# Seven block products for eight in 13 of 44 pairs of k-tiles of a down projection

## The chip, the core and the metric

The kernel runs on one core of one Trainium2 chip. The metric is the device time of one execution in microseconds. A core has TensorE (matrix products, results into PSUM), VectorE, ScalarE and GpSimd (POOL in the profile) for the other arithmetic, and SyncE, whose queue issues the loads. PSUM has eight banks of 128 x 512 float32 values each.

## The reference

One layer of an encoder block for 256 tokens of width 2048: a mixer, then a gated feed-forward part, then a gated per-layer embedding. The part that changes is the feed-forward part's second product:

```python
def conv_glu(hn, w_up, conv_w, conv_b, w_down):
    up = hn @ w_up
    gate, val = jnp.split(up, 2, axis=-1)
    gate = dwconv_centred(gate, conv_w, conv_b)
    return (jax.nn.gelu(gate, approximate=True) * val) @ w_down
```

`w_down` is 5632 x 2048. The product is 256 tokens by 5632 by 2048, in float32. Its result is normalised by row and added to the residual `h`; then `h`, normalised, is multiplied by `w_ple_gate` (2048 x 2048).

## The kernel before

Float32 products are made from three products of a rounded type (float32r). Each operand is split into a high part (a cast) and a low part (the operand less its high part), and the result is high x high + high x low + low x high. So every block product is three matmuls. The helper `split` (lines 138 to 149) does this for weights: a ScalarE cast into a tile `whi` (names ending in `h`) and a VectorE subtraction into a tile `wlo` (names ending in `l`). There are five buffers of each, and a buffer comes free when TensorE has read it.

The weights come as raw tiles `raw` (lines 151 to 154) of 128 x 2048 values, two k-tiles of 1024 columns, one load of 1 MB each through SyncE's queue, into three buffers. A k-tile is 128 rows of the weight matrix.

The down projection is `sublayer("dn", w_down, ...)` (line 749). It runs over two halves of 1024 output columns. For each half it has four PSUM banks `acc[t][n]`: t is the block of 128 tokens, n the block of 512 columns. They are named `dna` in the profile. `token_major` (lines 201 to 221) runs over 22 pairs of k-tiles. For each it loads the raw tile, splits the two k-tiles and makes 24 matmuls: two k-tiles x two token blocks x three products x two column blocks. They go k-tile by k-tile, except in the last pair, where they go bank by bank, so that the banks end one after the other. `get_hid` (line 730) splits the hidden activations of a pair into a tile `hs` (two buffers): one ScalarE cast and one VectorE subtraction of 512 columns.

At the end of a half each bank is squared and summed by ScalarE (`dnj`, line 669) and multiplied by the gain into the pages `dnm` by VectorE (line 670). After the second half the row factors are worked out on POOL, `h` is updated (line 677), turned by TensorE into PSUM (`dnxt`), and split into `dnxh` and `dnxl` (lines 183 and 184). That panel is the input of the gate product. Between the down projection and the gate stands a small product `ple` of 24 matmuls (line 752).

PSUM is given out from two pools: six banks tagged `main` and two tagged `misc`. The pages of 128 x 2048 values have 13 buffers and the tiles `mid` of 128 x 1024 have three.

The order of the instructions on each engine isn't written out. A scheduler takes the program as the code traces it and sets each engine's order by its own estimates of time, so an instruction may stand earlier or later than in the code. On the chip each engine then takes its instructions strictly in that order.

Of the kernel before, what the change touches and what calls it, by code (L numbers as in the profile page):

```python
# [11 lines left out]
F32 = mybir.dt.float32  # L12
F32R = mybir.dt.float32r
# [3 lines left out]
P = 128  # L17
L = 256
# [5 lines left out]
NF = DFF // P  # L24
# [13 lines left out]
V_FCW, V_PN, V_FCB, V_N = 120, 252, 268, 312  # L38
# [13 lines left out]
def build(nc, a, out):  # L52
    x = a["x"][0]
    w_in, w_out, w_up = a["w_in"][0], a["w_out"][0], a["w_ffn_up"][0]
    w_down, w_gate, w_ple = a["w_ffn_down"][0], a["w_ple_gate"][0], a["w_ple"][0]
    out = out[0]

    with tile.TileContext(nc) as tc, \
# [8 lines left out]
        def ins(r):  # L67
            return getattr(r, "ins", r)

        def page(name, dtype=F32):  # L70
            return gp.tile([P, 2048], dtype, tag="pg", bufs=13, name=name)

        def mid(name, dtype=F32):
            return gp.tile([P, 1024], dtype, tag="mid", bufs=3, name=name)

        def tiny(name, n=2):
            return sp.tile([P, n], F32, tag="tiny", bufs=40, name=name)

        def main(name):
            return [pm.tile([P, 512], F32, tag="main", name=f"{name}_{i}") for i in range(2)]  # L80

        def misc(name):
            return pc.tile([P, 512], F32, tag="misc", name=name)

        def mm(o, lhsT, rhs, start, stop):
            nc.tensor.matmul(o, lhsT, rhs, start=start, stop=stop, skip_group_check=True)  # L86
# [17 lines left out]
        acc, acc2 = [main(f"dtu{t}") for t in range(2)], main("dtu2")  # L104
# [10 lines left out]
        def load(dst, src, ahead=False):  # L115

            with tc.issue_after(last["dma"]) if last and not ahead else nullcontext():
                return ins(nc.sync.dma_start(dst, src))
# [19 lines left out]
        def split(name, src, nel, cuts=()):  # L138

            if name in spare:  # L140
                hi, lo = spare.pop(name)
            else:
                hi = wp.tile([P, 1056], F32R, tag="whi", bufs=5, name=f"{name}h")
                lo = wp.tile([P, 1056], F32R, tag="wlo", bufs=5, name=f"{name}l")
            for c0, c1 in zip((0, *cuts), (*cuts, nel)):
                s = slice(c0, c1)
                last["act"] = ins(nc.scalar.copy(hi[:, s], src[:, s]))
                last["dve"] = ins(nc.vector.tensor_sub(lo[:, s], src[:, s], hi[:, s].bitcast(F32)))  # L148
            return hi, lo

        def raw(name, src, a_, b_):
            r = wp.tile([P, 2048], F32, tag="raw", bufs=3, name=name)
            last["dma"] = load(r[:, :a_ * b_].rearrange("p (a b) -> p a b", a=a_), src, True)
            return r
# [34 lines left out]
        def aside():  # L189

            for job in (work.pop(0) if work else ()):
                job()

        def columns(acc):

            c = 0
            for o in acc:
                yield o, c
                c += o.shape[-1]

        def token_major(name, w, c0, ks, get, acc, tail=1):

            group, nu = [], len(ks) // 2
            for u in range(nu):
                k0 = ks[2 * u]
                r = raw(f"{name}r{k0}", w[k0 * P:(k0 + 2) * P, c0:c0 + 1024]
                        .rearrange("(k p) c -> p k c", p=P), 2, 1024)
                for j in range(2):
                    group.append((k0 + j, *split(f"{name}{k0}_{j}", r[:, j * 1024:(j + 1) * 1024], 1024)))
                if nu - tail <= u < nu - 1:  # L210
                    continue

                order = [(t, o, g, q) for t in range(2) for o in columns(acc[t]) for g in group for q in range(3)] \
                    if u == nu - 1 else \
                    [(t, o, g, q) for g in group for t in range(2) for q in range(3) for o in columns(acc[t])]
                for t, (o, c), (k, wh, wl), q in order:
                    xh, xl = (v[:, t * P:(t + 1) * P] for v in get(k))
                    xx, ww = ((xh, wh), (xh, wl), (xl, wh))[q]
                    mm(o, xx, ww[:, c:c + o.shape[-1]], k == ks[0] and q == 0, k == ks[-1] and q == 2)
                group = []  # L220
                aside()

# [39 lines left out]
        def rms(name, parts, scale, n=1):  # L262

            base = EPS
            for i, q in enumerate(parts):
                m = tiny(f"{name}m{i}", n)
                nc.gpsimd.tensor_scalar(m, q, scale, base, op0=ALU.mult, op1=ALU.add)
                base = m
            r = tiny(f"{name}r", n)
            nc.gpsimd.tensor_tensor(r, m, mhalf[:, :n], op=ALU.pow)  # L270
            return r
# [71 lines left out]
        for u in range(0, NK, 2):  # L343
            r = [wp.tile([P, 2048], F32, tag="raw", bufs=3, name=f"dtur{u}") if u else r0, page(f"dtur{u + 1}")]
            for j in range(2):
                k = u + j
# [17 lines left out]
            for j in range(2):  # L364
                k = u + j
                with tc.issue_after(front[0]), tc.issue_after(front[1]):
                    wh, wl = split(f"dtu{k}", r[j][:, :1056], 1056, ((352, 704), (704,))[k] if k < 2 else ())
                if k == 8:
                    half = last["act"], last["dve"]
# [241 lines left out]
        ])  # L611
        zacc = [main(f"z{t}") for t in range(2)]
        token_major("z", w_in, 0, list(range(NK)), hn, zacc)
        assert not work

# [4 lines left out]
        for t in range(2):  # L620
# [13 lines left out]
            r = rms(f"yn{t}", [ss], rz[t][:, 1:2], n=2)  # L634
# [16 lines left out]
        def gload(name, src):  # L651
            g = cp.tile([P, D], F32, tag="gain", name=name)
            load(g, src.partition_broadcast(P))
            return g

        def sublayer(name, w, ks, get, gain, h, vnext, panel=Panel):

            mg = [page(f"{name}m{t}") for t in range(2)]
            sq = [[], []]
            for half in range(2):  # L660
                acc = [main(f"{name}a{half}{t}") for t in range(2)]
                token_major(f"{name}{half}", w, half * 1024, ks, get, acc)
                for t in range(2):
                    for n in range(2):
                        q = tiny(f"{name}q{t}{half}{n}", 1)
                        junk = sp.tile([P, 512], F32, tag="junk", bufs=1, name=f"{name}j{t}{half}{n}")
                        c = slice(half * 1024 + n * 512, half * 1024 + (n + 1) * 512)
                        b = acc[t][n]
                        nc.scalar.activation(junk, b, AF.Square, accum_out=q)
                        nc.vector.tensor_mul(mg[t][:, c], b, gain[:, c])  # L670
                        sq[t].append(q)
            r = [rms(f"{name}{t}", sq[t], 1.0 / D) for t in range(2)]
            pan = panel(f"{name}x")
            for c in range(4):
                s = slice(c * 512, (c + 1) * 512)
                for t in range(2):
                    nc.vector.scalar_tensor_tensor(h[t][:, s], mg[t][:, s], r[t], h[t][:, s],  # L677
                                                   op0=ALU.mult, op1=ALU.add)
                panel_part(f"{name}x", pan, h, vnext, 4 * c, 4 * c + 4)
            return pan  # L680
# [15 lines left out]
        h = [page(f"h{t}") for t in range(2)]  # L696
# [9 lines left out]
        hid = [page(f"hid{i}") for i in range(6)]  # L706
        for s in range(DFF // 512):
            sc = mid(f"gr{s}")
            for i in range(2):
                ga = main(f"ga{s}{i}")  # L710
                feature_pairs(f"ug{s}{i}", w_up, s * 512 + i * 256, hf, ga)
                o = sc[:, i * 512:(i + 1) * 512]
                total(o, ga)
                v = o.rearrange("p (f t) -> p f t", f=2)
# [5 lines left out]
            for i in range(2):  # L720
                va = main(f"va{s}{i}")
                feature_pairs(f"uv{s}{i}", w_up, DFF + s * 512 + i * 256, hf, va)
                c0 = (s % 2) * 1024 + i * 512
                hd = hid[s // 2][:, c0:c0 + 512]
# [5 lines left out]
        def get_hid(k):  # L730
            if k % 2 == 0:
                t = lp.tile([P, 1024], F32R, tag="hs", bufs=2, name=f"hs{k}")
                src = hid[k // 8][:, (k % 8) * L:(k % 8 + 2) * L]
                nc.scalar.copy(t[:, :512], src)  # L734
                nc.vector.tensor_sub(t[:, 512:], src, t[:, :512].bitcast(F32))
                cur["t"] = t
            o = (k % 2) * L
            return cur["t"][:, o:o + L], cur["t"][:, 512 + o:512 + o + L]
# [3 lines left out]
        def hid_get(k):  # L742
# [3 lines left out]
                hcache[k0], hcache[k0 + 1] = get_hid(k0), get_hid(k0 + 1)  # L746
            return hcache[k]

        hp = sublayer("dn", w_down, list(range(NF)), hid_get, gload("gffn", a["ffn_norm_post"][0]), h, V_PN)


        pl.append(ple(1))
# [32 lines left out]
        for half in range(2):  # L785
            acc = [main(f"gt{half}{t}") for t in range(2)]
# [9 lines left out]
            for t in range(2):  # L796
                for n, (o, c0) in enumerate(columns(acc[t])):
                    c1 = c0 + o.shape[-1]
                    c = slice(half * 1024 + c0, half * 1024 + c1)

                    th = mid(f"gth{half}{t}{n}")
                    v = th[:, :c1 - c0]
# [6 lines left out]
                    q = tiny(f"gq{t}{half}{n}", 1)  # L809
# [53 lines left out]
```

## Time and profile before

| | |
|---|---|
| median of three runs | 1154.63 us (1154.47 to 1155.65) |
| the profiled execution's own time | 1154.53 us |
| its span, first to last instruction | 1152.5 us |
| mean granted TensorE clock | 0.995 |
| TensorE matmuls busy | 1134.8 us |
| VectorE busy | 753.5 us |
| ScalarE busy | 574.7 us |
| down projection, from its first matmul to the next stage's | 800.7 to 1044.75 us |
| loads of a raw tile of `w_down`, issue to landing | 5.5 and 5.6 us |

The profile gives for each engine how long it was busy, and for each instruction when it started, how long it lasted and what ended the idle time before it. PE is TensorE's matmuls, PEld its weight loads, DVE is VectorE, ACT is ScalarE. Instructions of one engine overlap at their ends, so the distance from one start to the next is a little less than the duration shown. A matmul of 128 x 512 is shown with 0.39 us, but in a full stretch one starts every 0.231 us.

### The profile page before, as it was taken

How to read it: one execution, taken by the hardware profiler on the slowest of the kernel's cores; microseconds unless marked ns; L12 is line 12 of the kernel's file. 1: busy time of each engine (PE TensorE's matmuls, PEld its weight loads, DVE VectorE, ACT ScalarE, POOL GpSimd, SP SyncE). 2: the span in 40 equal slices, each digit the busy share in tenths (PEclk: the TensorE clock that was granted, in tenths of full speed). 3: DMA queues.
4: the chain of work that ended last, by engine and by line, in shares of the span. 5: the costliest groups of instructions: out<-in, count | busy, mean ns of one | idle time of the engine just before them, and what ended most of it. 6: DMA issues, size and time to landing. Idle time of an engine off the chain costs nothing.

```text
span 1152.5 us, 15287 instructions
## 1 busy us (share of the span) xinstructions
PE 1134.8 (98%) x6096; PEld 978.4 (85%) x6096; DVE 753.5 (65%) x934; ACT 574.7 (50%) x775; POOL 121.4 (11%) x123
## 2 busy tenths in 40 slices
PE   9998999999999999999999999999999999999996
PEld 9997988888888888888888888888888888887886
DVE  6578896654776666666666766766555565557573
ACT  6533543553675454554544544545444454447462
POOL 0274505200110000000000000000000000001001
PEclk9998999999999999999999999999999999999999
DMA  9952357556456555556555555566666656664652
GB/s 355 337 182 75 109 163 275 184 161 204 144 186 215 186 183 184 191 192 195 189 183 183 188 194 196 183 208 202 187 193 196 191 183 187 191 193 160 221 181 73
DMA packets 129590, 219.02 MB, mean 190 GB/s; under 512 B 3696, under 2 KB 96752, under 8 KB 128624
## 3 DMA queue, kind: packets, MB, share of 16 engines
q1 hardware_dynamic: 129232, 217.70, 57.9%
q8 instruction: 47, 0.77, 0.3%
q10 hardware_dynamic: 288, 0.36, 0.1%
q14 instruction: 23, 0.19, 0.0%
HBM read 215.95 MB, written 2.10 MB: 189 GB/s over the span
## 4 chain that ended last, share of the span: by engine, by line
PE 92%; DVE 5%; ACT 1%; issue 1%; POOL 1%; DMA 0%; DVEq 0%; POOLq 0%; ACTq 0%
PE va L86 21%; PE dna L86 21%; PE ga L86 21%; PE woa L86 8%; PE gt L86 7%; PE dtu L86 4%; PE z L86 4%; PE xbc L86 3%; DVE cv L328 2%; DVE w L541 1%; DVE xb_0l L148 1%; PE ple L86 0%; PE yd L86 0%; DVE h L677 0%; DMA dtur<-w_in 0%
## 5 line engine op out<-in xcount | busy, mean ns | idle before, releaser
L86 PE MATMUL ga<-wox,ug_0h 128*128 128x512 f32 x352 | 125.5, 395 | 0.0
L86 PE MATMUL ga<-wox,ug_1h 128*128 128x512 f32 x352 | 125.1, 394 | 0.0
L86 PE MATMUL va<-wox,uv_0h 128*128 128x512 f32 x352 | 124.8, 393 | 0.0
L86 PE MATMUL va<-wox,uv_1h 128*128 128x512 f32 x352 | 124.8, 393 | 0.0
L86 PE MATMUL dna<-dn_1h,hs 128*128 128x512 f32 x352 | 104.4, 393 | 0.0
L86 PE MATMUL dna<-dn_0h,hs 128*128 128x512 f32 x352 | 104.4, 393 | 0.0
L86 PE MATMUL ga<-wox,ug_0l 128*128 128x256 f32 x352 | 99.1, 282 | 0.0
L86 PE MATMUL ga<-wox,ug_1l 128*128 128x256 f32 x352 | 99.1, 282 | 0.0
L86 PE MATMUL va<-wox,uv_0l 128*128 128x256 f32 x352 | 99.1, 281 | 0.0
L86 PE MATMUL va<-wox,uv_1l 128*128 128x256 f32 x352 | 99.1, 281 | 0.0
L86 PEld LDWEIGHTS dna<-dn_1h,hs 128*128 128x128 f32 x352 | 66.1, 188 | 15.3
L86 PEld LDWEIGHTS dna<-dn_0h,hs 128*128 128x128 f32 x352 | 66.0, 188 | 15.3
L86 PEld LDWEIGHTS va<-wox,uv_0h 128*128 128x128 f32 x352 | 66.1, 188 | 15.0
L86 PEld LDWEIGHTS va<-wox,uv_1h 128*128 128x128 f32 x352 | 66.1, 188 | 15.0
L86 PEld LDWEIGHTS ga<-wox,ug_1h 128*128 128x128 f32 x352 | 66.1, 188 | 14.9
L86 PEld LDWEIGHTS ga<-wox,ug_0h 128*128 128x128 f32 x352 | 66.1, 188 | 14.8
L718 POOL TENSOR_TENSOR fc<-fc,rfb 128x1024 f32<-128x1024 f32 x11 | 26.4, 2404 | 440.1 <-ACT fc L717 440.1
L86 PEld LDWEIGHTS ga<-wox,ug_0l 128*128 128x128 f32 x352 | 66.2, 188 | 0.1
L86 PEld LDWEIGHTS ga<-wox,ug_1l 128*128 128x128 f32 x352 | 66.2, 188 | 0.0
L86 PEld LDWEIGHTS va<-wox,uv_1l 128*128 128x128 f32 x352 | 66.2, 188 | 0.0
L86 PEld LDWEIGHTS va<-wox,uv_0l 128*128 128x128 f32 x352 | 66.2, 188 | 0.0
L734 ACT CAST hs<-hid 128x512 fp32r<-128x512 f32 x44 | 27.3, 620 | 71.1 <-PE dna L86 70.7
(639 smaller groups left out, 2650.5 us busy)
## 6 DMA issues: line engine op xcount, KB each, us to landing
dn0r<-w_ffn_down SPq DMA_DIRECT2D x22, 1024.0 KB, 5.5
dn1r<-w_ffn_down SPq DMA_DIRECT2D x22, 1024.0 KB, 5.6
zr<-w_in SPq DMA_DIRECT2D x8, 1024.0 KB, 5.3
wo0r<-w_out SPq DMA_DIRECT2D x8, 1024.0 KB, 5.7
wo1r<-w_out SPq DMA_DIRECT2D x8, 1024.0 KB, 5.5
gt0r<-w_ple_gate SPq DMA_DIRECT2D x8, 1024.0 KB, 5.8
gt1r<-w_ple_gate SPq DMA_DIRECT2D x8, 1024.0 KB, 5.5
dtur<-w_in SPq DMA_DIRECT2D x14, 528.0 KB, 8.8
```

Of the source, the lines that this page charges most:

```text
L86: nc.tensor.matmul(o, lhsT, rhs, start=start, stop=stop, skip_group_check=True)
L148: last["dve"] = ins(nc.vector.tensor_sub(lo[:, s], src[:, s], hi[:, s].bitcast(F32)))
L328: nc.vector.scalar_tensor_tensor(o[:, lo:hi], i[:, lo + d:hi + d], vec(wcol + j * wstep + f), o[:, lo:hi], op0=ALU.mult, op1=ALU.add)
L541: nc.vector.scalar_tensor_tensor(w[:, h * P:(h + 1) * P], cbm[:, 0, g, t, :], dt[:, t, 8 * g + h:8 * g + h + 1], w[:, h * P:(h + 1) * P], ...
L718: nc.gpsimd.tensor_tensor(cv.rearrange("p (f t) -> p f t", f=4), cv.rearrange("p (f t) -> p f t", f=4), rfb.unsqueeze(1).to_broadcast([P, ...
L734: nc.scalar.copy(t[:, :512], src)
```

## The change

Two k-tiles, two blocks of 128 tokens and two blocks of 512 columns make a product of 2 x 2 blocks by 2 x 2 blocks. Done plainly it has eight block products. In 13 of the 44 pairs (pairs 2, 5, 8, 11, 14 and 17 of each half, and 19 of the second) the kernel after uses Strassen's scheme in Winograd's form, with seven block products. It needs sums and differences of the weight blocks and of the activation blocks.

- `seven_products` forms the weight sums in place in the raw tile by three VectorE subtractions, one 1024 and two 512 columns wide. It splits four pieces in place of two: `a` (512 columns), `b`, `c` and `d` (1024 each); `a` and `b` are taken before the subtractions change their blocks. Then it makes 7 x 3 matmuls. Three products go into the result banks `acc`; four go into four more banks `alt` (named `dns`), where they add up over all fast pairs of the half.
- `hid_sums` forms four sums of activation blocks by four VectorE operations on 128 x 128 values, and splits them (512 columns). For pairs 2, 5, 8 and 11 the split sums are kept in two pages `hsum` for the second half; the others are made in each half (`hd`, `he`).
- `combine` runs once in each half, in the pair after the last fast one. It adds the four shared banks into the result banks in place: one ScalarE copy and eight VectorE additions, four of them with a PSUM bank as input and output. That pair's matmuls go bank by bank, as the last pair's do.
- The banks: half 0 takes two of the six `main` banks and both `misc` banks for `alt`, beside the four of `acc`; half 1 likewise.

The rest of the code is as before. The scheduler sets the order anew. In its new order on VectorE the low split `gt_1l` of the gate's second k-tile stands behind six of the `dnxl` instructions; before it stood ahead of the last `dnm`. In SyncE's queue the load of `gple` stands ahead of the fourth load `gt0r` and not behind it.

```diff
+        def seven_products(name, r, a_, acc, alt, start, stop):
+            v = r.rearrange("p (b c) -> p b c", b=4)
+            b11 = split(f"{name}a", r[:, :512], 512)
+            b2 = split(f"{name}b", r[:, 1024:], 1024)
+            nc.vector.tensor_sub(v[:, 0:2], v[:, 1::2], v[:, 0:2])
+            nc.vector.tensor_sub(v[:, 3], v[:, 3], v[:, 0])
+            nc.vector.tensor_sub(v[:, 2], v[:, 2], v[:, 3])
+            t13 = split(f"{name}c", r[:, :1024], 1024)
+            t42 = split(f"{name}d", r[:, 1024:], 1024)
+            for x, (wh, wl), c, o, own in (
+                    ("a11", b11, 0, alt[0], True), ("a12", b2, 0, acc[0][0], False), ("s4", b2, 512, acc[0][1], False),
+                    ("s1", t13, 0, alt[1], True), ("s3", t13, 512, alt[2], True), ("a22", t42, 0, acc[1][0], False),
+                    ("s2", t42, 512, alt[3], True)):
+                xh, xl = a_[x]
+                for q, (xx, ww) in enumerate(((xh, wh), (xh, wl), (xl, wh))):
+                    mm(o, xx, ww[:, c:c + 512], own and start and q == 0, own and stop and q == 2)
+
+        def combine(name, acc, alt):
+            m = [mid(f"{name}v{i}") for i in range(2)]
+            p1, s16, s165, s167 = (m[i // 2][:, i % 2 * 512:(i % 2 + 1) * 512] for i in range(4))
...
+            nc.scalar.copy(p1, alt[0])
+            add(s16, alt[3], p1)
+            add(acc[0][0], acc[0][0], p1)
+            add(s165, alt[1], s16)
+            add(acc[0][1], acc[0][1], s165)
+            add(s167, alt[2], s16)
+            add(acc[1][0], acc[1][0], s167)
+            add(s165, alt[2], s165)
+            add(acc[1][1], acc[1][1], s165)
...
+                if u in fast:
+                    seven_products(f"{name}{k0}", r, sums(k0), acc, alt, u == fast[0], u == fast[-1])
+                    continue
...
-                    if u == nu - 1 else \
+                    if u == nu - 1 or u - 1 in fast[-1:] else \
...
+                if u - 1 in fast[-1:]:
+                    combine(name, acc, alt)
...
+                alt = main(f"{name}s{half}") if fast[half] and half == 0 else []
                 acc = [main(f"{name}a{half}{t}") for t in range(2)]
+                if fast[half]:
+                    alt += (main(f"{name}s{half}") if half else []) + [misc(f"{name}s{half}_{i}") for i in (2, 3)]
...
+        def hid_sums(k):
+            (h1, l1), (h2, l2) = get_hid(k), get_hid(k + 1)
+            if k not in kept:
...
+                nc.vector.tensor_add(s1, a21, a22)
+                nc.vector.tensor_sub(s3, a11, a21)
+                nc.vector.tensor_sub(s2, s1, a11)
+                nc.vector.tensor_sub(s4, a12, s2)
+                o = keep[-1][:, n % 2 * 1024:(n % 2 + 1) * 1024] if n < 4 else mid(f"he{k}", F32R)
+                nc.scalar.copy(o[:, :512], s[:, :512])
+                nc.vector.tensor_sub(o[:, 512:], s[:, :512], o[:, :512].bitcast(F32))
...
+        hp = sublayer("dn", w_down, list(range(NF)), hid_get, gload("gffn", a["ffn_norm_post"][0]), h, V_PN,
+                      fast=((2, 5, 8, 11, 14, 17), (2, 5, 8, 11, 14, 17, 19)), sums=hid_sums)
```

## The prediction

> **What bounds the kernel now.** I read four views, from the whole to the place of the change. First the engine table of the page, then the chain that ended last: TensorE is busy for 98% of the span and makes 92% of the chain.
>
> ```profile
> PE 1134.8 (98%) x6096; PEld 978.4 (85%) x6096; DVE 753.5 (65%) x934; ACT 574.7 (50%) x775; POOL 121.4 (11%) x123
> PE 92%; DVE 5%; ACT 1%; issue 1%; POOL 1%; DMA 0%; DVEq 0%; POOLq 0%; ACTq 0%
> ```
>
> Then what TensorE waited for in the whole kernel: seven waits, none of them in the down projection. The third lies just behind it, in the first gate matmuls.
>
> ```profile
> PE seg L86 <- DVE catl L184: 5.0, 1, 5.0
> PE gt L86 <- DVE gt_0l L148: 0.7, 1, 0.7
> ```
>
> The two halves of the down projection, in windows (TensorE, weight loads, VectorE, ScalarE, POOL, granted clock, DMA share, GB/s): TensorE never stops, at full clock, and VectorE works 70 of 122 us.
>
> ```profile
> 800.70:922.70 122.00, 122.00 (x530) 99.13 (x529) 70.32 (x70) 58.84 (x73) 0.90 (x2) 1.00 0.61 190
> 922.70:1044.70 122.00, 122.00 (x529) 99.11 (x529) 70.77 (x70) 59.59 (x74) 1.53 (x5) 1.00 0.61 190
> ```
>
> So here each matmul taken out is worth its spacing, as long as VectorE and ScalarE stay ahead. The timeline gives the spacing: the last pair starts at 1039.21 and the next stage's first matmul at 1044.75, 24 matmuls, 0.231 us each. In that pair six in a row go to one bank and are no slower, so three in a row in the new pairs cost nothing extra.
>
> ```profile
> 1039.21 0.39 PE L86 MATMUL dna<-dn_0h,hs 128*128 128x512 f32 x1
> 1044.75 0.40 PE L86 MATMUL ple<-ple_0h,pth 128*128 128x512 f32 x1
> ```
>
> The helpers' rows in the same stage: a 1024-wide VectorE subtraction lasts 1.23 us, and the next starts 1.14 after it (1067.31, 1068.44); a 512-wide one 0.69, next after 0.60. ScalarE's casts: 1.05 (next after 0.96) and 0.62 (0.53).
>
> **The change part by part.**
>
> *Matmuls.* A fast pair has 7 products of 3 matmuls, 21 for 24. 13 pairs make 39 fewer (the built program has 39 fewer): 39 x 0.231 = **-9.0 us**, all on the path.
>
> *A fast pair's helpers.* VectorE: three in-place subtractions (1.14 + 0.60 + 0.60), four low splits (0.60 + 3 x 1.14), the hidden split 0.60: 7.0 us, where an ordinary pair has 2 x 1.14 + 0.60 = 2.9. ScalarE: 0.53 x 2 + 0.96 x 3 = 3.9 for 2.5. TensorE gives it 4.85 us and an ordinary pair 5.54. So VectorE falls behind in a fast pair and recovers in the two ordinary ones: 7.0 + 2 x 2.9 = 12.8, some 13.0 with the waits on its own results, of 15.9 us. What counts is the lead. Splits have five buffers, so each may start when the one five before it has been read (ScalarE starts 0.2 after that). With zero at TensorE's start of a fast pair: next pair's splits done by 2.4 and 3.6, its hidden split by 4.2 (wanted at 5.8); the second's by 5.3, 6.4, 7.0; of the next fast pair a at 7.6, first subtraction 8.8, b 10.1, the other two 11.3, c 13.4, d 15.6. TensorE wants a at 15.9, c at 18.0, d at 19.4. Nearest margin 1.6 us, for d 3.8: cost 0. If that cover were gone, each late microsecond would come back 13 times.
>
> *DMA.* A raw tile is held until d is split, 0.3 us before its pair is consumed; the load three pairs on is issued then and lands at about 5.3 (median 5.5 to 5.6), used from 5.1, while a is wanted at 15.9: cost 0, and 0 at double. SP's order changes in one place, `gple` before the fourth `gt0r` load; that load now waits for the late `gt_1l` below, lands at about 17 and is split after 22: 0.
>
> *Hidden sums.* Nine times four 128x128 operations and one 512-wide, plus a cast. No such sum is in the trace: between 0.23 (the 128x128 copy) and 0.41 (256-wide add); I take 0.25, near the row of its width: 1.6 us each. In the built order they start during the last up-projection step, where VectorE stands idle up to 1.6 us at a time, and end by the first fast pair. The casts into `hsum` wait for pages of `wox` (about 793 and 796) and hold up ScalarE's `dn_1h` from 798.05 to 798.6, wanted at 809. Behind the sums the hidden split of the pair after the first fast one is ready at 816.2, wanted at 817.4: cost 0; at 0.41 the margin is about used up, still 0. The three sums of half 1 lie around the change of halves, ahead of its first fast pair: 0.
>
> *Combine.* Eight VectorE adds per half. Four write SBUF like `dnm` (0.69, next after 0.60); four write PSUM in place, which no row shows: from 0.60 (`dnm` only reads it) to 1.23 (a second pass, the 1024-wide row). I take 0.60. The first needs the fast pair's last product; the others wait for the bank-by-bank pair that follows, and VectorE's splits are queued behind. In the built order TensorE takes the other banks first: bank 1,1 is wanted 7.6 us after that pair begins and its add ends at 6.8; the next hidden split is wanted at 6.9 and ready at 6.25, in half 1 at 7.1 and 6.6. Cost 0, at 1.23 about 1.2 to 1.6 a half, **0 to +2.8**.
>
> *The seam behind it.* The built order moves `gt_1l` (1.14 on VectorE) from ahead of the last `dnm` to behind the sixth `dnxl`. Zero at the first full stretch of `ple` (1044.75 before). VectorE: last `dnm` to 1.9; four `h` of 0.66 to 4.6; two `dnxl` (0.39, waiting for `dnxh`) to 5.75; two `h` to 7.1; two `dnxl` behind ScalarE's `gt_1h` to 8.0; two `h` to 9.3; two `dnxl` to 10.1; `gt_1l` ends 11.3. TensorE: 23 `ple` and 8 transposes to 6.2, eight gate matmuls to 8.0, eight transposes of 0.088 to 8.74, then it needs `gt_1l`: until 11.38, **2.64 us**. The old wait there goes, as VectorE is past `gt_0l` before TensorE is; it cost 1056.59 - 1055.67 (four transposes from 1055.32) = 0.92. Net **+1.7**. Bounds: -0.9 without any wait, +2.5 if the `dnxl` come 0.8 later.
>
> ```profile
> 1055.32 0.60 PE L280 MATMUL dnxt<-ident,h 128*128 128x128 f32 x4
> 1056.59 0.72 PE L86 MATMUL gt<-gt_0l,dnxh 128*128 128x512 f32 x2 [0.67 <-DVE gt_0l L148]
> ```
>
> *Half change.* `dnm` of half 0 ends 2 us ahead of the matmul that needs its bank, though 2.5 us of sums go in ahead of it: 0. Behind the seam the order is the same to the end.
>
> Sum: -9.0 + 1.7 = -7.3. The profiled execution took 1154.53 (span 1152.5 and 2.0 around it), 0.1 under the median of 1154.63: **1147.3 us**.
>
> **The rivals.** Below 0.2% (2.3 us) a measurement of this kernel can't tell a change from none.
>
> *No wait at the seam:* VectorE's chain proves shorter, or TensorE slower to get there. -9.9: 1144.7. Against it: `gt_1l` stands behind six `dnxl` whose inputs come from TensorE itself. 7%.
>
> *The clock falls after the new gap.* The trace has two gaps to compare: after 0.67 us the clock stays 1.00, after 4.95 it is 0.60 and then 0.55 for eight us.
>
> ```profile
> 100.00:104.00 4.00, 1.20 (x3) 1.04 (x4) 3.40 (x7) 2.34 (x4) 0.00 (x0) 0.60 0.80 262
> 104.00:108.00 4.00, 4.00 (x12) 3.15 (x12) 2.34 (x4) 1.28 (x3) 0.70 (x1) 0.55 0.50 135
> ```
>
> A fall like that costs at most 4 x 0.40 + 4 x 0.45 = 3.4: 1150.7. 2.6 is nearer to 0.67. 7%. The Trainium skill, "TensorE: Matmul & The Clock Gate" (HAM oscillation), has the gate close only after gaps over about 3.4 us; by that rule there is no fall here, and the two gaps agree with it.
>
> *TensorE waits for the combine:* the in-place adds cost 1.23. +2.8: 1150.1. For it: all eight banks are held and no row shows the operation. Against: the PSUM read is free (0.69 in `dnm`, 0.69 in `hs`). 11%. The Trainium skill, "Perfetto Trace Analysis" (Optimizing Tensor Performance), wants matmul groups to rotate through banks so that one is emptied under the next; here the groups go on in the banks being added to, and by that rule this rival is the likely one. No row of this trace decides it; the built order gives TensorE other banks first.
>
> *VectorE becomes the bound, and the kernel slower.* Place: the fast pairs. 13.0 us of VectorE per 15.9: from 1.22 times dearer on TensorE waits, and from 1.27 times (0.56 a period, 13 periods) the 7.3 are gone. The trace has such a factor: `z_1l` takes 1641 ns, the same subtraction as `dn_1l` at 1226, 1.34 times. At 1.34, 13.0 grows to 17.4, 1.5 late in 13 periods: 1147.3 + 19 = 1166, less if the leads cushion it. Against: the long ones stand where POOL works, and POOL has 0.9 and 1.5 us in the down projection's halves; the change gives it nothing. 7%.
>
> That the change doesn't do what it says is excluded by the 39.
>
> **How the numbers follow.** Likeliest, seam wait and all else hidden: 63%, 1147.3. The cases above take 7, 7, 11 and 7%; 5% is several at once. The range reaches from no seam wait (1144.5) to past the clock's fall (1151.0) and leaves VectorE's case and the mixtures out. Faster 0.88 (all but those), same 0.05 (mixtures), slower 0.07.
>
> **What the profile after would show.** Right: TensorE solid from `dna`'s start to its end, the stage about 235 us long with 1017 matmuls; one wait of `gt` for `gt_1l` of 2.3 to 2.6 us in place of that for `gt_0l`; VectorE near 85% busy. Wrong: waits of `dns` or `dna` for low splits at every fast pair (VectorE), one per half for an add (combine), a clock under 1.00 after 1040, or several waits at the seam.

## The result and the profile after

The kernel after takes 1146.65 us (median, 1146.28 to 1147.28) where the kernel before takes 1154.58 (1154.47 to 1155.65). The ratio is 0.9931, 95% interval 0.9918 to 0.9943: 0.7% faster. The profiled execution of the kernel after took 1147.28 us, with a span of 1145.5; that is 7.25 us less than the profiled execution of before (1154.53), and the prediction was 7.3 less. Between the medians the difference is 7.9; the profiled execution is the slowest of the four.

The first two lines are from the engine table and the chain that ended last, of the kernel after. Then follow the two waits that matter in the list of TensorE's waits (total, number, longest):

```profile
PE 1126.3 (98%) x6057; PEld 971.6 (85%) x6057; DVE 824.8 (72%) x1060; ACT 598.3 (52%) x812; POOL 122.5 (11%) x123
PE 92%; DVE 5%; POOL 1%; ACT 1%; issue 1%; POOLq 0%; DVEq 0%; ACTq 0%
...
PE seg L86 <- DVE catl L184: 4.9, 1, 4.9
PE gt L86 <- DVE gt_1l L148: 2.2, 1, 2.2
```

TensorE is still the bound. The down projection has no wait in the list. The wait behind it has changed from `gt_0l` (0.7) to `gt_1l` (2.24; the forecast for this line was 2.3 to 2.6). Windows over the down projection of the kernel after (TensorE, weight loads, VectorE, ScalarE, POOL, granted clock, DMA share, GB/s):

```profile
801.08:860.00 58.92, 58.92 (x257) 47.85 (x256) 51.26 (x64) 33.30 (x42) 0.00 (x0) 1.00 0.54 179
860.00:918.27 58.27, 58.27 (x254) 47.38 (x253) 51.02 (x64) 35.40 (x47) 0.90 (x2) 1.00 0.67 217
918.00:977.00 59.00, 59.00 (x257) 47.96 (x256) 50.59 (x59) 34.59 (x44) 0.00 (x0) 1.00 0.54 178
977.00:1036.19 59.19, 59.19 (x258) 48.08 (x257) 52.11 (x60) 36.74 (x48) 1.38 (x4) 1.00 0.61 198
```

The second column of times is TensorE: it is busy in every microsecond. VectorE went from 58% to 87% (205.0 of 235.4 us).

Where the time went is best read by stages. TensorE's matmuls ahead of the down projection are the same, in the same order, in all kernels here, yet its first matmul started anywhere from 800.1 to 802.2 us in the profiles of this study. So effects under 1 us are read from two stretches of each trace: from the start of the first `dna` matmul to the start of the last, and from there to the end of the span (the seam to the gate, the gate, and the end).

| | before | after | difference |
|---|---|---|---|
| start of the down projection | 800.74 | 801.08 | +0.34 |
| first to last matmul of it | 243.77 | 234.87 | -8.90 |
| from its last matmul to the end | 107.99 | 109.55 | +1.56 |
| span | 1152.5 | 1145.5 | -7.0 |

One of the 24 `ple` matmuls moved into the last pair, so 0.23 belongs to the other row: the down projection lost 9.13 and the stretch behind it gained 1.79. With the moved `ple` matmuls counted alike, the stretch behind is 109.55 to 109.68 in the four profiles whose program is the same from there on (after, and `ktile_order`, `sub2` and `pool_sums` below).

### The profile page after: what moved, and what is told of

Same layout as the page of the kernel before. It is cut to its first block, busy times and chain, and to the rows that moved or that the text cites. A ratio compares the mean times of both kernels' runs of the same rounds, so it can differ in the third digit from the quotient of the medians.

```text
span 1145.5 us, 15408 instructions
## 1 busy us (share of the span) xinstructions
PE 1126.3 (98%) x6057; PEld 971.6 (85%) x6057; DVE 824.8 (72%) x1060; ACT 598.3 (52%) x812; POOL 122.5 (11%) x123
## 4 chain that ended last, share of the span: by engine, by line
PE 92%; DVE 5%; POOL 1%; ACT 1%; issue 1%; POOLq 0%; DVEq 0%; ACTq 0%
PE va L86 21%; PE ga L86 21%; PE dna L86 17%; PE woa L86 8%; PE gt L86 7%; PE dtu L86 4%; PE z L86 4%; PE xbc L86 3%; PE dns L86 3%; DVE cv L373 2%; DVE w L586 1%; DVE xb_0l L148 1%; PE ple L86 1%; PE yd L86 0%; DVE h L726 0%
## 5 line engine op out<-in xcount | busy, mean ns | idle before, releaser
L86 PE MATMUL dna<-dn_0h,hs 128*128 128x512 f32 x248 | 75.8, 393 | 0.0
L86 PE MATMUL dna<-dn_1h,hs 128*128 128x512 f32 x248 | 75.6, 393 | 0.0
L86 PEld LDWEIGHTS dna<-dn_1h,hs 128*128 128x128 f32 x248 | 46.5, 188 | 10.8
L86 PEld LDWEIGHTS dna<-dn_0h,hs 128*128 128x128 f32 x248 | 46.5, 188 | 10.7
L86 PE MATMUL dna<-dn_0l,hs 128*128 128x512 f32 x124 | 40.2, 393 | 0.0
```

## The experiments

Lengths below are those two stretches. For the kernel after they are 234.87 and 109.55.

**Half of the change.** The second half of the down projection as before:

```diff
-                      fast=((2, 5, 8, 11, 14, 17), (2, 5, 8, 11, 14, 17, 19)), sums=hid_sums)
+                      fast=((2, 5, 8, 11, 14, 17), ()), sums=hid_sums)
```

> The six fast pairs of the first half alone; the second half as in the kernel before. VectorE's order at the gate is then the old one (gt_1l ahead of the last dnm). Theory (each matmul taken out is worth its spacing, the seam costs by gt_1l's place alone): 18 matmuls x 0.231 = -4.2 and nothing at the seam, 1154.6 - 4.2 = 1150.4; one wait of gt for gt_0l of about 0.7 as before, none in the down projection. Rival (the fast pairs themselves carry a hidden price, and the sum of 7.3 came out by chance): the first half is shorter by less than 4.0 us, and the time is above 1150.8.

Measured: 1150.17 us (1149.66 to 1150.7), ratio 0.9966 (0.9955 to 0.9978). The two stretches are 239.57 and 108.27. In its list of TensorE's waits the seam is the old one again:

```profile
PE gt L86 <- DVE gt_0l L148: 0.7, 1, 0.7
```

The down projection is 4.20 shorter for 18 matmuls, 0.233 each. The price of a matmul is right, and nothing that comes with six fast pairs shows in that stage. The stretch behind it is 0.3 longer than before; VectorE's `gt_1l` starts 0.2 later there, behind a wait for ScalarE.

**The combine without its own order.** The pair behind the last fast one goes k-tile by k-tile:

```diff
-                    if u == nu - 1 or u - 1 in fast[-1:] else \
+                    if u == nu - 1 else \
```

> The pair after the last fast one goes k-tile by k-tile like the others, not bank by bank; nothing else changes. Theory (the combine is hidden only because the order of that pair frees the banks one after the other): in the k-tile order no bank is finished before the 18th of 24 matmuls, four of the adds are left when the pair ends, and TensorE wants bank 1,0 again 1.4 us later, with two or three adds of 0.6 still to run: 1 to 2 us of waiting in each half, +2 to +4, 1148.6 to 1150.6; waits of dna for an add in place. Rival (the adds are short enough to be hidden in any order): no wait, 1146.6.

Measured: 1148.0 us (1146.46 to 1148.59); the stretches are 234.73 and 109.91. There is no wait for an add: the rival holds. The median is 1.35 above that of after, but the two stretches together are 344.64 against 344.42. In the profiled execution the difference lies ahead of the down projection, which began at 802.16 (801.08 in after); the full clock came 3.7 us later at the start of this execution. VectorE's timeline behind the first half's last fast pair in this run shows why. The pair began at 897.80, the next at 903.35:

```profile
898.33 0.68 DVE L228 TENSOR_TENSOR dn0v<-dns,dn0v 128x512 f32<-128x512 f32 x1
...
900.06 1.28 DVE L228 TENSOR_TENSOR dn0v<-dns,dn0v 128x512 f32<-128x512 f32 x2
...
901.93 2.08 DVE L228 TENSOR_TENSOR dna<-dna,dn0v 128x512 f32<-128x512 f32 x3
903.92 0.68 DVE L228 TENSOR_TENSOR dn0v<-dns,dn0v 128x512 f32<-128x512 f32 x1
...
905.65 0.69 DVE L228 TENSOR_TENSOR dna<-dna,dn0v 128x512 f32<-128x512 f32 x1
```

Three adds in place run under the end of the pair; the first result bank is done at about 902.6 and wanted at 903.35. The fourth add ends at 906.3. The built order of TensorE puts that bank's matmuls late in the next pair (three with `dn_0` are left for 906.81), so it isn't waited for either. An add with PSUM as input and output takes 0.69 us, and the next starts 0.60 after it, the price of the row that only reads PSUM; the third of the three in 2.08 us had to wait 0.08 for its bank's last product. The Trainium skill, "Perfetto Trace Analysis" (Optimizing Tensor Performance), has groups of matmuls rotate through banks so that one is emptied while the next is filled; here all eight banks are held and emptied in place, and neither order made TensorE wait.

**The seam: `gt_1l` moved back.** The splits of the pair of `ple` and of the gate's first pair are traced behind the last matmul of the down projection:

```diff
                 token_major(f"{name}{half}", w, half * 1024, ks, get, acc, 1, fast[half], alt, sums)
+                if name == "dn" and half == 1:
+                    for key, src in (("ple1r0", w_ple), ("gt0r0", w_gate)):
...
+                            early_split[n] = split(n, g[:, j * 1024:(j + 1) * 1024], 1024)
```

> The kernel after, with the splits of ple's pair and of the gate's first pair traced right behind the down projection's last matmul, ahead of its dnm: gt_1l then stands ahead of the last two dnm in VectorE's order. Theory (the seam's 2.6 us come from the place of gt_1l alone): the wait for gt_1l goes, VectorE's later work comes some 1 us later and an old wait of about 0.9 for gt_0l comes back: -1.7, 1145.0. Rival (VectorE has the same work between the last dna and the gate in any order, so the wait only changes its name): a wait of 2 us or more for another operand, 1146.6.

In a second kernel the gate's second k-tile is also given a page of its own, so that its split needs no buffer of the last pair:

```diff
+                    s0 = page("gt00", F32R)
+                    spare["gt00_1"] = (s0[:, :1024], s0[:, 1024:])
```

> As gate_early, and the gate's second k-tile is split into a page of its own, so that this split need not wait for the last down-projection pair to release a buffer: VectorE makes it during the last pair, where it has 2 us to spare. Theory: VectorE's chain behind the last dna gets 1.14 us shorter, neither wait stays: -2.6, 1144.1 (down to 1143.9, up to 1145.0 if a wait for gt_0l of the second pair is left). Rival (the wait only changes its name): 1146.6.

Measured: 1146.74 us (1146.19 to 1147.42) and 1146.24 (1146.08 to 1146.79). The stretches behind the last matmul are 109.38 and 109.35, against 109.55. My theory of the place of `gt_1l` falls; the wait changed its name: in both kernels one of 2.24 became two of 1.2 and 0.4. TensorE's timeline in the second of these kernels:

```profile
1044.18 1.04 PE L326 MATMUL dnxt<-ident,h 128*128 128x128 f32 x8
...
1047.55 1.07 PE L326 MATMUL dnxt<-ident,h 128*128 128x128 f32 x8 [1.19 <-DVE dnxl L184]
1048.99 0.72 PE L86 MATMUL gt<-gt_0l,dnxh 128*128 128x512 f32 x2 [0.37 <-DVE gt_0l L148]
```

The transposes go in eights, into two PSUM banks at once, so the next eight wait until VectorE and ScalarE have emptied both. In the kernel before they go in fours, with gate matmuls between.

**The seam: the old order pinned.** First on VectorE and ScalarE alone, with edges that only fix the order (H is an update of `h`, X a `dnxl`, the figure behind it the k-tile):

```diff
+        chain("Dgt00_0 dD00 dD01 dD10 Dgt00_1 dD11 H00 H01 H10 H11 X0 X2 H20 X1 H21 X3 H30 X4 H31 X5 X6 Dgt02_0 X7 X8 Dgt02_1 "
+              "X9 X10 Dgt04_0 X11")
+        chain("dA00 dA01 dA10 Agt00_1 dA11 Agt02_0 A0 A2 A1 Agt02_1 A3 Agt04_0 A4 A6 A5 A7 A8 P00 P01 A9 A10 P10 P11 A11")
```

> The kernel after, with VectorE's and ScalarE's order between the last dnm and the gate's third pair pinned to that of the kernel before: gt_1l ahead of the last dnm, and the dnxl taken bank by bank (each dnxt bank emptied before the next), not two banks side by side; so TensorE's transposes go in fours again, not in eights. New theory (gate_early showed that gt_1l's place alone only renames the wait; what costs is the whole order, the two dnxt banks emptied together): from the last dna matmul to the end of the span 108.0 as in the kernel before and in half0, not 109.5 as in after and gate_early: -1.5, 1145.1. Rival (VectorE comes late into the seam because of the fast pairs of the second half, which half0 lacks, and no order mends it): 109.5 again, 1146.6.

And the same with the gate's second k-tile in a page of its own:

> As seam_old, and the gate's second k-tile split into a page of its own ahead of the first dnm, so that 1.14 us of VectorE's chain lie under the last pair. Theory: the old wait for gt_0l goes too, 107.1 from the last dna matmul to the end, 0.9 under seam_old: 1144.2. Rival (that wait is set by the transposes and ScalarE's casts, not by VectorE): 108.0, 1145.1.

Measured: 1148.18 us (1146.22 to 1148.56) and 1148.57 (1146.5 to 1149.29). The stretches are 111.07 and 111.31, longer than after. Most of that isn't the order: behind the waits TensorE ran at half clock for 3.4 us, which is taken up below. It was busy all that time, so the half clock cost 1.7, and without it the stretches would be 109.4 and 109.6 (an estimate), about that of after. TensorE's own order had not been pinned: its first transposes stood behind 20 `ple` matmuls instead of 14 and began 4.9 us after the last `dna` matmul, where the kernel before begins at 3.5.

Then on all three engines:

```diff
+        chain([pe[int(i)] for i in (
+              '32 33 34 35 36 37 38 39 40 41 42 43 44 45 0 4 46 47 1 2 3 5 6 7 48 49 50 51 52 53 '
...
+              "Dgt00_0 dD00 dD01 dD10 Dgt00_1 dD11 H00 H01 H10 H11 X0 X2 H20 X1 H21 X3 H30 X4 H31 X5 X6 Dgt02_0 X7 X8 "
```

> The kernel after, with the order of all three engines (TensorE too, which seam_old left as it was) between the last dna matmul and the gate's third pair pinned to that of the kernel before: four transposes after three gate matmuls, and so on. Same instructions, same work. Theory (the seam costs by the whole order, above all by TensorE's transposes standing too late, which makes the dnxl and then gt_1l late): 108.0 to 108.3 us from the last dna matmul to the end, as in before and half0, against 109.5: 1145.2. Rival (VectorE comes late into the seam from the fast pairs of the second half): 109.5 or more, 1146.6.

Measured: 1146.36 us (1145.9 to 1146.54), ratio 0.9929 (0.9916 to 0.9943). The stretch is 108.81: with the old order 0.74 of the 1.56 come back, and 0.82 stay (1.05 of the 1.79 with the moved `ple` matmul). Both theories are half right. What stays is seen in VectorE's timeline at the end of the down projection. In the kernel before, whose last `dna` matmul starts at 1044.51:

```profile
1040.49 1.23 DVE L148 TENSOR_TENSOR gt_0l<-gt0r,gt_0h 128x1024 fp32r<-128x1024 f32 x1 [1.54 <-ACT gt_0h L147]
1041.64 0.68 DVE L670 TENSOR_TENSOR dnm<-dna,gffn 128x512 f32<-128x512 f32 x1
...
1045.33 1.23 DVE L148 TENSOR_TENSOR gt_1l<-gt0r,gt_1h 128x1024 fp32r<-128x1024 f32 x1 [0.29 <-ACT gt_1h L147]
```

In the pinned kernel, whose last `dna` matmul starts at 1035.29:

```profile
1033.52 1.22 DVE L150 TENSOR_TENSOR gt_0l<-gt0r,gt_0h 128x1024 fp32r<-128x1024 f32 x1
1034.65 1.88 DVE L725 TENSOR_TENSOR dnm<-dna,gffn 128x512 f32<-128x512 f32 x3
1036.45 1.22 DVE L150 TENSOR_TENSOR gt_1l<-gt0r,gt_1h 128x1024 fp32r<-128x1024 f32 x1
...
1039.37 0.75 DVE L732 SCALAR_TENSOR_TENSOR h<-dnm,dn1r,h 128x512 f32<-128x512 f32 x1 [0.44 <-POOL dn1r L318]
```

`gt_0l` starts 4.0 us ahead of the last matmul before and 1.8 ahead in the pinned kernel. VectorE still works off the last fast pair (pair 19 of 22) and the combine, without idle time, and reaches `gt_1l` 0.34 later (1.16 after the last matmul against 0.82). Another 0.44 is a wait for the row factor `dn1r` from POOL, which came later too (4.0 us behind the last matmul against 2.8). Together 0.78 of the 0.82.

**VectorE's margin.** Two of the 1024-wide low splits in every fast pair are made twice:

```diff
             t13 = split(f"{name}c", r[:, :1024], 1024)
             t42 = split(f"{name}d", r[:, 1024:], 1024)
+            for hi, lo, o in ((*t13, 0), (*t42, 1024))[:2]:
+                nc.vector.tensor_sub(lo[:, :1024], r[:, o:o + 1024], hi[:, :1024].bitcast(F32))
```

> The kernel after, with two of the 1024-wide low splits of each fast pair (of c and d) made twice, same values: +2.28 us of VectorE in each of 13 fast pairs, nothing else. VectorE is idle 7.7 of the first 58.9 us of the down projection, 2.1 a period of three pairs. Theory (the helpers are hidden by a margin of about 2 us a period, and each late microsecond comes back 13 times): 0.2 late a period, up to 0.6 where the leads run out: +2 to +8, 1149 to 1155, with waits of dns or dna for low splits. Rival (TensorE follows VectorE already, the margin isn't there): +2.28 x 13 = 30, 1176. Other rival (the five buffers hold a lead that never runs out): 0.

Measured: 1154.3 us (1152.62 to 1155.6), ratio 0.9996 (0.9987 to 1.0005): the whole gain is gone, as the theory had it (1149 to 1155). The profiled execution is the fastest of ten. In it the down projection is 241.26 long, +6.4 for 29.6 us of added VectorE work, so some 23 us of it were hidden. The waits are those of VectorE's results:

```profile
PE dna L86 <- DVE hs L786: 1.3, 3, 0.5
PE dna L86 <- DVE dna L230: 1.1, 1, 1.1
PE dns L86 <- DVE dn138cl L215: 1.0, 1, 1.0
```

The second line is an add in place: where the margin is spent, the combine is waited for too.

**POOL beside VectorE.** The four 128x128 sums of hidden blocks on POOL:

```diff
-                nc.vector.tensor_add(s1, a21, a22)
+                nc.gpsimd.tensor_add(s1, a21, a22)
...
```

> The kernel after, with the four 128x128 sums of hidden blocks on POOL in place of VectorE: 36 operations. It tests the price that the prediction took from z_1l (1641 ns against 1226 where POOL works). If POOL slows VectorE, the 1024-wide subtractions beside these operations take up to 1.64 us, those apart from them 1.22; 0.8 us less on VectorE a fast pair against some 1 us more in the subtractions that they meet: hidden, 1146.6. If POOL doesn't slow it, all stay at 1.22: 1146.6 too; the rows decide, not the time.

Measured: 1147.66 us (one run); the stretches are 235.46 and 109.62. The rows decide, as said. VectorE's and POOL's timelines of this run:

```profile
796.40 1.53 DVE L148 TENSOR_TENSOR dn_0l<-dn0r,dn_0h 128x1024 fp32r<-128x1024 f32 x1 [0.29 <-ACT dn_0h L147]
808.94 1.48 DVE L148 TENSOR_TENSOR dn04bl<-dn0r,dn04bh 128x1024 fp32r<-128x1024 f32 x1
814.00 1.23 DVE L148 TENSOR_TENSOR dn04dl<-dn0r,dn04dh 128x1024 fp32r<-128x1024 f32 x1
```

```profile
806.97 1.50 POOL L814 TENSOR_TENSOR hd<-hd,hid 128x128 f32<-128x128 f32 x1
801.42 0.46 POOL L813 TENSOR_TENSOR hd<-hid 128x128 f32<-128x128 f32 x1
```

Beside POOL's sums the subtraction takes 1.53 and 1.48 us instead of 1.22, and the sums take up to 1.50 instead of 0.46. So the rival's price was real (1.21 to 1.25 times), and it stays away in the down projection of the kernel after, where POOL works only 2.3 us in all. The down projection got 0.6 longer: the one wait listed is for the `hs` split of the pair behind the first fast one (0.3), the place that the prediction had as its narrowest.

**More fast pairs.** Eight in each half, then the same with the seam pinned, then nine in each half, pinned:

```diff
-                      fast=((2, 5, 8, 11, 14, 17), (2, 5, 8, 11, 14, 17, 19)), sums=hid_sums)
+                      fast=((2, 4, 7, 9, 12, 14, 17, 19), (2, 4, 7, 9, 12, 14, 17, 19)), sums=hid_sums)
```

> Eight fast pairs in each half (2, 4, 7, 9, 12, 14, 17, 19), 16 in place of 13: 9 fewer matmuls, -2.1. VectorE per five pairs: 2 x 7.0 + 3 x 2.9 + 2 x 1.4 of sums = 25.5 of the 26.3 us that TensorE takes. Theory (VectorE still just keeps up): 1144.6. Rival (it falls behind in the two fast pairs that have one pair between them; by the same arithmetic 14.0 + 2.9 + 1.4 = 18 in 15.2 us): some 1 us of waiting per such place, up to +8: 1146 to 1152.

> Eight fast pairs in each half as in fives (the down projection took 233.0 us there, with no wait in it), and the seam's order pinned as in pinned. Theory: 233.0 + 108.2, 1143.3, and no time at half clock behind the seam, since no gap over 1.3 us is left. Rival (pinning doesn't hold the seam, or the half clock comes after any gap): 1144.5 to 1146.

> Nine fast pairs in each half (every second one from 2 to 18), the seam's order pinned as in pinned: 15 fewer matmuls than after, -3.5. VectorE per two pairs: 7.0 + 2.9 + 1.4 of sums (half of them kept in the second half) = 11.3 of the 10.4 us that TensorE takes. Theory (here VectorE becomes the bound): 0.9 late a period where sums are made, up to 13 periods, less the leads: +5 to +10 of waits, the down projection 236 to 241 us, 1146 to 1151. Rival (the lead hides it): 231.4 us, 1141.7.

| | median us (range) | ratio to before | down projection | behind it |
|---|---|---|---|---|
| after (13 pairs) | 1146.65 (1146.28 to 1147.28) | 0.9931 (0.9918 to 0.9943) | 234.87 | 109.55 |
| 16 pairs | 1146.18 (1145.34 to 1146.96) | 0.9927 (0.9913 to 0.9940) | 233.0 | 111.26 |
| 16 pairs, pinned | 1144.31 (1144.08 to 1145.02) | 0.9913 (0.9899 to 0.9926) | 232.79 | 109.31 |
| 18 pairs, pinned | 1145.45 (1145.17 to 1145.72) | 0.9922 (0.9908 to 0.9935) | 235.46 | 107.98 |

With 16 pairs TensorE still never waits in the down projection, though two fast pairs have one ordinary pair between them: the rival of 1 us at each such place is refuted; that the lead of five buffers carries it is the likely reason, not a tested one. Nine fewer matmuls gave 1.87 (2.1 forecast). With the seam pinned, 108.2 was forecast behind the stage and 109.31 came, for the reasons found in the pinned kernel: VectorE reaches `gt_1l` 0.76 later than before and waits 0.44 for `dn1r`, together 1.20 of the 1.32. With 18 pairs VectorE is the bound in places: 15 fewer matmuls than after, yet the stage is 0.6 longer, 4.0 us over the 231.5 that its matmuls need (4.5 to 9.5 by the theory, 0 by the rival). The two listed waits of this run in that stretch:

```profile
PE ple L88 <- ACT ple_0h L149: 1.9, 1, 1.9
PE dna L88 <- DVE dna L231: 1.3, 1, 1.3
```

The first comes from VectorE in a roundabout way. ScalarE's cast `ple_0h` waited for its load, and that load was issued at 1018.30, when VectorE's split `dn_1l` (1017.05 to 1018.27) had let go of a raw tile:

```profile
1024.92 1.04 ACT L149 CAST ple_0h<-ple1r 128x1024 fp32r<-128x1024 f32 x1 [0.88 <-DMA ple1r<-w_ple]
```

The run with 18 pairs also completes the reading of the seam. Its last fast pair is 18, not 19, and VectorE's `gt_0l` again starts 4.0 us ahead of the last matmul (1031.81 against 1035.82). With the pinned order and VectorE on time the stretch is 107.98, that of the kernel before. TensorE's wait of 1.9 us at 1026 helped VectorE to be on time, so the place of the last fast pair isn't tested alone.

The best version is the one with 16 pairs, pinned: 2.3 us under the kernel after by the medians, and 2.3 by the two stretches (342.10 against 344.42). The intervals of the two ratios overlap; the runs were not made side by side.

## Why the prediction was right, step by step

That 7.25 meets 7.3 so closely is partly luck: the profiled execution of after lost 0.34 ahead of the down projection and gained some 0.25 outside its span. The stages are the better test: -9.13 + 1.79 = -7.34.

*Matmuls, -9.0.* Right: -9.13 in the whole change, -4.20 (-4.16 by the prediction's price) in half of it. Groups of three in one bank cost nothing.

*A fast pair's helpers, 0.* Right. VectorE's rows are those the sum used. The margin was real, but smaller than said: 13.0 of 15.9 us a period would let TensorE wait from 1.22 times. The first window above has VectorE busy 51.26 of 58.92 us, 13.8 a period, because the hidden sums, which the prediction priced apart, fall into the same periods: waiting starts at 1.15 times. 2.3 more make 16.1, just past 15.9, and that made TensorE wait.

*Hidden sums, 0.* Right. An operation of 128x128 took 0.29, the next start 0.20 behind it (0.25 was taken), a little cheaper than thought. The trace of before had a nearer row than those used: `cbm`, 128x128, 0.285. One sum met POOL's `fc` (786.84 to 789.25) and took almost nine times as long; it was far enough ahead of the first fast pair to cost nothing:

```profile
786.89 2.51 DVE L813 TENSOR_TENSOR hd<-hid 128x128 f32<-128x128 f32 x1
```

The narrowest place was where the prediction had it: the hidden split behind the first fast pair was ready at 817.06 and wanted at 817.95. A margin of 0.9 against a forecast 1.2.

*Combine, 0.* The value is right, and so is the price of 0.60 to 0.69 for an add in place. One reason given for it isn't needed: the prediction had the bank-by-bank order of that pair protect TensorE. Without that order nothing waited.

*The seam, +1.7.* The sum is right to 0.1 (+1.79), down to the time at which `gt_1l` ends: 11.35 us behind the start of `ple`'s full stretch, 11.3 forecast. Shown by TensorE's timeline of the kernel after:

```profile
1044.31 1.03 PE L325 MATMUL dnxt<-ident,h 128*128 128x128 f32 x8
1047.59 0.72 PE L86 MATMUL gt<-gt_1l,dnxh 128*128 128x512 f32 x2 [2.24 <-DVE gt_1l L148]
```

The gap behind the eight transposes is 2.58 us, 2.64 was forecast. The cause behind the number was named too narrowly. The text laid it to the place of `gt_1l` in VectorE's order. Moving it back gained 0.2. What costs is, in about equal parts, the order of all three engines (transposes in eights into two banks: 0.74) and a VectorE that enters the seam late after the last fast pair and the combine (0.82). The adding up was right because it walked through the built order instruction by instruction, with VectorE's backlog in it as "last `dnm` to 1.9" (1.94 measured). One part of it is luck: it has VectorE wait some 0.4 for `dnxh` ahead of 5.75. There is no such wait; VectorE waits 0.44 for `dn1r` a little earlier, which the prediction doesn't have, and the two cancel (5.90).

*Rivals.* VectorE as the bound, by POOL's neighbourhood: real in price, absent in the down projection of the kernel after. The factor of 1.34 was read from a mean that mixes rows of 1.22 with rows beside POOL, which are 2.4 times as long; in before:

```profile
179.22 2.92 DVE L148 TENSOR_TENSOR z_1l<-zr,z_1h 128x1024 fp32r<-128x1024 f32 x1 [1.79 <-ACT z_1h L147]
```

TensorE waiting for the combine: refuted here. The clock after the new gap: not in the profile of after, but it does come in others, as the last section shows, at 1.7 us and not the 3.4 of the bound. It fell in one of five profiles with such a wait, and the 7% was too low a chance for it.

*The +0.34 ahead of the down projection* is in no step; it comes from the granted clock between 104 and 112 us (0.72 in this execution, 0.77 in that of before), in code that both share.

## What to carry to other kernels

Where one engine is the bound and has no gaps, taking out its work is worth its spacing, and the question is only whether the helpers keep ahead: count them per period, and look for the narrowest place behind a burst. A wait at a seam need not be due to the instruction it names; move that instruction, and the wait changes its name unless the chain that feeds it gets shorter or the whole order changes. When more work is put on a helper engine, keep it away from the last few microseconds ahead of a seam where that engine becomes the bound.

## What was not expected of the hardware

**The clock can fall after a gap of 2.6 us.** The kernel after and the one with 16 pairs have the same gap at the seam, 2.58 and 2.57 us from the eighth transpose, counted at its spacing, to the next matmul (the waits listed are 2.24 and 2.23). In the profile of after the granted clock stays 1.00. In that of the 16 pairs it falls to half, which makes the stretch behind the down projection 1.7 us longer (111.26 against 109.55). The kernels with the order pinned on two engines fell too, after two waits in a row of 1.3 and 0.8, and of 1.5 and 0.8 us. Four profiles with a wait for `gt_1l` of 2.2 to 2.4 us show no fall, that of the kernel after among them.

The traces show what decides. In each of the fourteen profiles the clock's changes lie whole multiples of 3.413 us apart; with 16 pairs they come at 102.69, 106.10, 1044.77 and 1048.18, that is 1, 275 and 1 of these steps. Windows laid on the steps (TensorE's busy time is the second figure, the granted clock the third from the right): 16 pairs, then after, then the order pinned on VectorE and ScalarE.

```profile
1041.36:1044.77 3.41, 1.26 (x10) 0.92 (x8) 3.41 (x7) 2.36 (x5) 0.00 (x0) 1.00 0.00 0
1044.77:1048.18 3.41, 3.33 (x12) 2.94 (x13) 2.23 (x5) 0.47 (x1) 0.00 (x0) 0.50 0.67 184
```

```profile
1043.66:1047.08 3.42, 1.69 (x12) 1.27 (x10) 3.42 (x7) 2.80 (x6) 0.00 (x0) 1.00 0.00 0
1047.08:1050.49 3.41, 2.90 (x17) 2.28 (x17) 3.34 (x7) 1.48 (x4) 0.00 (x0) 1.00 0.47 134
```

```profile
1046.53:1049.94 3.41, 1.31 (x7) 1.00 (x8) 3.14 (x7) 2.46 (x6) 0.00 (x0) 1.00 0.00 0
1049.94:1053.36 3.42, 3.42 (x12) 2.74 (x11) 3.17 (x6) 2.29 (x6) 0.00 (x0) 0.50 0.27 62
```

With 16 pairs nearly the whole wait lies in one step; in after the end of a step at 1047.08 cuts it into 1.73 and 0.51. Over all steps of the fourteen profiles, from the first full clock to the last matmul, the clock fell behind each one in which TensorE was idle for 2.10 us or more (17 of them, 14 at about 100 us) and behind none with 1.73 or less; nothing lies between. The steps stand at another place of the program in each execution, so the same wait can fall either way. By an estimate from these figures, a wait of 2.24 us makes the clock fall at four to six of ten places. The fall at about 100 us lasted one step in five profiles, whose down projection began at 800.1 to 800.4, and two steps in the other nine (800.2 to 802.2).

The Trainium skill, "TensorE: Matmul & The Clock Gate" (HAM oscillation), gives gaps over about 3.4 us as what throttles; 2.6 sufficed here. The Trainium skill, "TensorE: Matmul & The Clock Gate" (What's actually happening), has the monitor look at a window of some 3.4 us that runs freely; the steps of 3.413 us agree with it. A seam without such a gap, as in the kernels pinned on all three engines, kept the clock at 1.00.

**POOL and VectorE slow each other,** even over operations of 128x128: 1.22 to 1.53 us for a subtraction, 0.46 to 1.50 for a sum. Beside 1024-wide operations of POOL it is more: 2.92 for the subtraction.

**An add in place in PSUM costs no more than a read of PSUM:** 0.69 us for 128x512.
